# A batched matrix product on one core: what GpSimd's loads wait for, and who tells VectorE that a set of accumulators is done

## The chip, the cores and the metric

The kernel runs on one core of one Trainium2 chip. A core has several engines, each with its own program: TensorE (PE) multiplies, VectorE (DVE) and ScalarE (ACT) copy and convert here, GpSimd (POOL) and SyncE (SP) issue transfers. The engines meet only through semaphores: one engine counts a semaphore up, another waits until it has reached a value. Transfers between the chip's memory (DRAM) and the on-chip memory (SBUF) run on 16 DMA engines. Matrix products land in accumulators (PSUM banks). The metric is the time of one execution on the device in microseconds (us).

## What is computed

The reference multiplies 32 independent pairs of matrices:

```python
def setup_inputs():
    batch, m, k, n = 32, 512, 1024, 768
    return {
        "x": np.random.randn(batch, m, k).astype(np.float32),
        "weight": np.random.randn(batch, k, n).astype(np.float32),
    }

def reference(x, weight):
    return np.matmul(x, weight).astype(np.float32)
```

Per batch that is 2.10 MB of x, 3.15 MB of weights and 1.57 MB of output, all float32. The whole problem reads 167.77 MB and writes 50.33 MB. Every byte is moved once.

## The kernel before

The 32 batches go in 16 pairs. For each pair k the kernel loads x of both batches (one transfer, `load_x`, L108 to L112) and the weights of both (one transfer, `load_w`, L93 to L98; the first four and the last two batches one at a time, L102). These loads convert float32 to bfloat16 on the way into SBUF. There are two slots for x (`X_SLOTS`), four for weights (two pairs), and four for the output of a pair. Only x of pair 0 comes in float32, on SyncE's queue, and is converted by VectorE and ScalarE.

TensorE's loop (`on_pe`) does, for each pair: the transposes of x (`transposes`, eight groups `g` through two PSUM buffers `pt`), then for each of the two batches four row tiles `mt` of 128 rows (`multiply`). A row tile is 8 steps `ko`, and each step is two matmuls: one of 512 columns (L167) and one of 256 columns (L140). Two neighbouring row tiles, an even and an odd one, make a set: they share three PSUM banks, bank 0 (512 columns of the even tile), bank 2 (512 columns of the odd tile) and bank 1 (256 columns of each). There are two sets of banks, p = 0 and p = 1, so a batch is two sets and a pair is four. TensorE waits at L182 (`take`) for x (`s_xr`) and for weights (`s_wr`), and through `await_copies` for the copies that empty the banks (`s_a`, `s_d`).

ScalarE's program (`out_on_act`) copies, for each set: bank 0 in two pieces, after the even tile (L264 to L267), then half of bank 2, after the odd one (L268, L269). Between the two sets of an odd batch it waits until the next pair's x has landed and passes that on to TensorE (`landed`, L338). Before a pair it waits for its output slot (`slot_free`).

VectorE's program copies, for each set (`set_on_dve`, L271 to L276), bank 1 in two pieces, and then the other half of bank 2. It also spreads the transposed x from PSUM into SBUF (`spreads`, L224 or, for the last pair, L232). Its order is fixed in its loop: the eight spreads of pair k, then the second set of the last batch of pair k-1, then the other three sets of pair k. So the last copy of a pair stands behind the spreads of the next.

The semaphores that the change touches:

- `s_mm` counts finished tiles for ScalarE. Before, an even tile counts it at its last matmul (L171), and an odd tile at the last matmul of 512 columns (L170).
- `s_set` tells VectorE that a set is complete. Before, TensorE counts it at the last matmul of an odd tile (L171). VectorE waits for it at L272 and counts it down.
- `s_dp` counts VectorE's finished sets, two for each batch, and `s_ap` ScalarE's.

GpSimd's program (`on_pool`, L345 to L369) is one list in a fixed order: after the first loads, for k = 0 to 13: x of pair k+2, the store of pair k-2 (from k = 2 on), then the weights of pair k+2. All these transfers use one queue. Before, the load of x for pair k+2 waits (L111) until VectorE has finished the four sets of each pair before pair k (for k = 0: its first set), and the load of the weights (L96) until VectorE has finished pair k altogether. A wait on GpSimd holds all that stands behind it in the list. SyncE passes on the landed weights and does the last stores: pair 14 in one transfer, the last two batches in halves.

The functions that the change touches, with the line numbers of the profile:

Of the kernel before, what the change touches and what calls it, by code (L numbers as in the profile page):

```python
# [12 lines left out]
def kernel(  # L13
# [12 lines left out]
    KT = K // P  # L26
# [6 lines left out]
    W_SLOTS, X_SLOTS, OUT_SLOTS = 4, 2, 4  # L33

    pe, dve, act, pool, sp = nc.tensor, nc.vector, nc.scalar, nc.gpsimd, nc.sync
# [25 lines left out]
    def sem(name):  # L61
        sems.append(nc.alloc_semaphore(name))
        return sems[-1]
# [5 lines left out]
    s_pt, s_c, s_mm, s_set = sem("s_pt"), sem("s_c"), sem("s_mm"), sem("s_set")  # L69
    s_free = sem("s_free")  # L70
    s_a, s_ap, s_d, s_dp = sem("s_a"), sem("s_ap"), sem("s_d"), sem("s_dp")
    s_st = [sem(f"s_st{i}") for i in range(OUT_SLOTS)]
    s_fin = sem("s_fin")

    def out_done(b):
        return 2 * (b + 1)

    def out_before(k):  # L80
        return 4 * k

    def last_out(b):

# [5 lines left out]
    def together(b):  # L90
        return W_SLOTS <= b < B - 2

    def load_w(b):  # L93
        if together(b):
            if b % 2 == 0:
                pool.wait_ge(s_dp, out_done(b + 1 - W_SLOTS))  # L96
                slots = all_ws[:, b // 2 % 2].rearrange("p r ko n -> p r (ko n)")
                pool.dma_start(out=slots, in_=w_two_view[b // 2]).then_inc(s_w[b % W_SLOTS], 16)  # L98
            return
        if b >= W_SLOTS:  # L100
            pool.wait_ge(s_dp, out_done(b - W_SLOTS))
        pool.dma_start(out=ws[b % W_SLOTS], in_=w_view[b]).then_inc(s_w[b % W_SLOTS], 16)  # L102

    def loads_of_w(b):
# [2 lines left out]

    def load_x(k):  # L108
        if k >= X_SLOTS:

            pool.wait_ge(s_dp, max(out_before(k - X_SLOTS), 1))  # L111
        pool.dma_start(out=xs[k % X_SLOTS], in_=x_view[k]).then_inc(s_x[k % X_SLOTS], 16)  # L112

    def copied(eng, j):
# [14 lines left out]
    def stationary(b, mt):  # L129
        return both[mt][:, b % 2].rearrange("p j h i r -> p j (h i) r")  # L130
# [7 lines left out]
    def other(out, weights, moving, first, last):  # L138

        return pe.add_instruction(  # L140
            mybir.InstMatmult(
                name=nc.get_next_instruction_name(),
                engine=mybir.EngineType.PE,
                ins=[pe.lower_ap(moving), pe.lower_ap(weights)],
                outs=[pe.lower_ap(out)],
                start_tensor_calc=first,
                stop_tensor_calc=last,
                tile_size=(P, P),
                tile_position=(0, 0),
                ldweights=False,  # L150
            )
        )

    def multiply(b, mt, w):
        pm, half = pms[mt // 2], mt % 2
        xT = stationary(b, mt)
        for ko in range(KT):
            for i, (bank, at, off, size) in enumerate(SPLITS[half]):
                args = (
                    pm[bank][:, at:at + size],  # L160
                    xT[:, ko // 2, :, ko % 2],
                    w[:, ko, off:off + size],
                )
                if i:
                    last = other(*args, ko == 0, ko == KT - 1)
                else:
                    full = pe.matmul(*args, start=(ko == 0), stop=(ko == KT - 1))  # L167

        if half:
            full.then_inc(s_mm, 1)  # L170
        last.then_inc(s_set if half else s_mm, 1)  # L171

    def transpose(k, g):

# [21 lines left out]
    def on_pe():  # L196


        odd = pe.alloc_register("odd")
        pe.reg_mov(odd, 0)  # L200
        pe.wait_ge(s_ident, 1)
        with nc.Fori(0, PAIRS, engines=[mybir.EngineType.PE], hint_back_edge=True):
            take(s_xr)
            for k in range(X_SLOTS):
                with pe.If_eq(odd, k):
                    transposes(k)
            w_pair = all_ws[:, bass.ds(nc.snap(odd, min_val=0, max_val=1), 1)]
            for b in range(2):
                take(s_wr)
                for mt in range(MT):  # L210
                    if b == 0:
                        await_copies(s_c, 2 * mt + 2, GROUPS, GROUPS)
                    at = 2 * b + mt // 2 + 1 + mt % 2
                    await_copies(s_a, at, 5, 4)
                    await_copies(s_d, at, 5, 4)
                    multiply(b, mt, w_pair[:, 0, b])
            pe.reg_alu(odd, odd, 1, mybir.AluOpType.bitwise_xor)
# [17 lines left out]
    def slot_free(a):  # L235

        if a >= OUT_SLOTS:
            act.wait_ge(s_st[a % OUT_SLOTS], 16 * (a // OUT_SLOTS)).then_inc(s_free, 1)
# [8 lines left out]
    def pieces(b, p, i):  # L247

        pm = pms[p][i]
        if i == 1:  # L250
            pm = pm.rearrange("p (t n) -> p t n", t=2)
        rows = [slice(0, H), slice(H, P)]
        at = p * N2
        if b >= B - 2:
            return [(columns(last_out(b)[half, at:at + N2], i), pm[half]) for half in rows]
        mine = outs[(b // 2) % OUT_SLOTS][H * (b % 2):H * (b % 2 + 1)]
        starts = [at + h * ROW for h in range(2)]
        return [(columns(mine[:, at:at + N2], i), pm[half]) for at, half in zip(starts, rows)]

    def out_on_act(b, p):  # L260
        j = 2 * b + p
        if b % 2 == 0 and p == 0:
            slot_free(b // 2)
        act.wait_ge(s_mm, 2 * j + 1)  # L264
        for piece in pieces(b, p, 0):
            last = act.copy(*piece)  # L266
        last.then_inc(s_a, 1)  # L267
        act.wait_ge(s_mm, 2 * j + 2)  # L268
        act.copy(*pieces(b, p, 2)[0]).then_inc(s_ap, 1)  # L269

    def set_on_dve(b, p):  # L271
# [60 lines left out]
    def on_act():  # L332
        act.sem_inc(s_a, 2)
        cast_first(act, act.copy, range(MT, 2 * MT)).then_inc(s_xr, 1)
        for b in range(B):
            out_on_act(b, 0)
            if b % 2 and b < B - 1:
                landed(act, s_x[(b // 2 + 1) % X_SLOTS], (b // 2 + 2) // 2, s_xr)  # L338
            out_on_act(b, 1)
# [5 lines left out]
    def on_pool():  # L345
        load_w(0)
        pool.memset(ident, 0.0).then_inc(s_zero, 1)  # L347
        pool.wait_ge(s_zero, 1)
        pool.affine_select(  # L349
            out=ident,  # L350
            in_=ident,
            compare_op=mybir.AluOpType.not_equal,
            fill=1.0,
            base=0,
            pattern=[[-1, P]],
            channel_multiplier=1,
        ).then_inc(s_ident, 1)
        load_w(1)
        load_x(1)
        load_w(2)  # L360
        load_w(3)
        for k in range(PAIRS - 2):
            load_x(k + 2)
            if k >= 2:
                store(pool, k - 2, s_st[(k - 2) % OUT_SLOTS])
            load_w(2 * k + 4)
            load_w(2 * k + 5)
        for a in range(PAIRS - 2 - HELD, PAIRS - 2):
            store(pool, a, s_st[a % OUT_SLOTS])  # L369
# [59 lines left out]
```

## Time and profile before

| what | value |
|---|---|
| time, median of 3 runs | 517.16 us (516.54 to 518.05) |
| the profiled execution's own time | 517.05 us |
| its span (first to last instruction) | 515.3 us |
| mean granted clock of TensorE | 0.945 |
| TensorE busy with matmuls | 429.7 us (83%) |
| VectorE busy | 212.9 us (41%) |
| ScalarE busy | 116.4 us (23%) |
| GpSimd busy | 28.9 us (6%) |
| GpSimd's queue, share of the 16 DMA engines' time | 95.1% |
| weight loads of a pair, issue to landing (median) | 30.9 us |
| x loads, issue to landing (median) | 39.8 us |
| stores, issue to landing (median) | 47.0 us |

How to read the profile's lines. The page cuts the span into 40 slices; a digit is the busy share of a slice in tenths. A window's line gives the stretch in us, the sum of its length, the busy time of each engine (with the number of instructions), the clock granted to TensorE (1 is full speed), the share of time that the 16 DMA engines were busy, and the GB/s that they moved, counted as bytes written; a load that halves its data counts half of what it reads. The share can be a little over 1, as transfers overlap. A timeline's line gives the start and the length in us, the engine and the line of the kernel, the operation, what it writes and reads, how often, and in brackets how long the engine had been idle before it and what ended that. A line of waits names the waiting engine and line, what it waited for, the total in us, how many times, and the longest. PEq and DVEq are the instruction queues of TensorE and VectorE, and L182 and L272 the lines of the waits in them.

### The profile page before, as it was taken

To read this page: it belongs to the slowest core of one execution; us is meant where nothing else is said; L and a number is where in the kernel's file an instruction comes from. 1 tells how busy PE (TensorE), PEld (TensorE's weight loads), DVE (VectorE), ACT (ScalarE), POOL (GpSimd) and SP (SyncE) were. 2 spreads that over 40 slices of the span, in tenths; PEclk is the share of its full clock that TensorE was granted. 3 is DMA by queue.
4 is the path that set the end of the run, shared out by engine and by line. 5 is a ranking of instruction groups with operands and counts; after the bars stand their busy time and mean duration, and the time that the engine had idled before them with its cause. 6 is when DMAs were issued, how large, how long until landed. Compare 5 with 4: busy or idle time off the path is not lost. (4 is left out here: it accounts for less than half of the span.)

```text
span 515.3 us, 5719 instructions
## 1 busy us (share of the span) xinstructions
PE 429.7 (83%) x2512; PEld 174.5 (34%) x1536; DVE 212.9 (41%) x332; ACT 116.4 (23%) x197; POOL 28.9 (6%) x54
## 2 busy tenths in 40 slices
PE   0299999999896896979969699795997969879991
PEld 0143425352434233342433423333242343422420
DVE  0343736364545144362444514535244353533631
ACT  0313131313131230312303123130221303113130
POOL 2000001010100001001010000101001010010000
PEclk9999999999999897998989979998898989979996
DMA  8999998999999999999999999999999999999997
GB/s 297 258 215 224 191 220 175 219 243 292 219 336 223 270 276 225 331 222 298 250 221 336 214 322 232 230 324 217 337 217 257 298 221 335 222 264 283 344 433 293
DMA packets 9444, 136.36 MB, mean 265 GB/s; under 512 B 864, under 2 KB 864, under 8 KB 1376
## 3 DMA queue, kind: packets, MB, share of 16 engines
q0 software_dynamic: 8576, 125.83, 95.1%
q1 hardware_dynamic: 864, 10.49, 4.9%
q14 instruction: 3, 0.02, 0.0%
q8 instruction: 1, 0.02, 0.0%
HBM read 167.77 MB, written 50.33 MB: 423 GB/s over the span
## 5 line engine op out<-in xcount | busy, mean ns | idle before, releaser
L167 PE MATMUL pm<-w,xT 128*128 x976 | 335.6, 393 | 0.0
L140 PE MATMUL pm<-w,xT 128*128 x1024 | 287.4, 281 | 41.2 <-PEq L182 35.7
L167 PEld LDWEIGHTS pm<-w,xT 128*128 128x128 bf16 x1024 | 103.3, 101 | 280.5 <-issue 279.8
L274 DVE COPY outs<-pm 64x512 f32<-64x512 f32 x128 | 88.1, 689 | 206.1 <-DVEq L272 204.7
L266 ACT COPY outs<-pm 64x512 f32<-64x512 f32 x128 | 74.2, 580 | 285.4 <-PE pm L140 284.7
L178 PE MATMUL pt<-ident,x 128*128 128x128 f32 x512 | 84.9, 309 | 33.1 <-PEq L182 22.8
L224 DVE COPY xT<-pt 128x1024 bf16<-128x1024 bf16 x120 | 77.7, 687 | 64.4 <-PE pt L178 64.3
L178 PEld LDWEIGHTS pt<-ident,x 128*128 128x128 f32 x512 | 71.5, 210 | 48.4 <-issue 26.2
L269 ACT COPY outs<-pm 64x512 f32<-64x512 f32 x64 | 37.0, 578 | 85.3 <-PE pm L167 85.3
L276 DVE COPY outs<-pm 64x512 f32<-64x512 f32 x64 | 43.9, 687 | 0.0
L98 POOL DMA_DIRECT2D w<-in_weight_dram x13 | 9.2, 706 | 362.5 <-DVE outs L276 362.5
L284 DVE CAST x<-outs 128x1024 bf16<-128x1024 f32 x4 | 2.5, 686 | 18.6 <-DMA outs<-in_x_dram 18.6
L112 POOL DMA_DIRECT2D x<-in_x_dram x15 | 8.3, 556 | 32.8 <-DVE outs L276 32.8
L284 ACT CAST x<-outs 128x1024 bf16<-128x1024 f32 x4 | 3.9, 1040 | 16.3 <-DMA outs<-in_x_dram 16.3
L120 POOL DMA_DIRECT2D out_dram<-outs x14 | 7.5, 539 | 0.1
L232 DVE COPY xT<-pt 128x512 bf16<-128x512 bf16 x16 | 5.7, 417 | 4.1 <-PE pt L178 4.1
L102 POOL DMA_DIRECT2D w<-in_weight_dram x6 | 3.4, 566 | 29.9 <-DVE outs L276 28.7
L284 ACT ACT_TABLE_LOAD x1 | 1.3, 1283 | 1.0 <-ACTq L391 1.0
L349 POOL TENSOR_SCALAR_AFFINE_SELECT ident<-ident 128x128 f32<-128x128 f32 x1 | 0.3, 284 | 0.2 <-POOL ident L347 0.2
L347 POOL MEMSET ident<- 128x128 f32 x1 | 0.2, 224 | 0.0
L413 POOL MEMSET const-float32-0.0<- 128x1 f32 x1 | 0.1, 100 | 0.2 <-issue 0.2
L413 POOL MEMSET const-bfloat16-1.0<- 128x1 bf16 x1 | 0.1, 103 | 0.0
(2 smaller groups left out, 0.2 us busy)
## 6 DMA issues: line engine op xcount, KB each, us to landing
out_dram<-outs POOLq DMA_DIRECT2D x14, 3072.0 KB, 47.0
w<-in_weight_dram POOLq DMA_DIRECT2D x13, 3072.0 KB, 30.9
x<-in_x_dram POOLq DMA_DIRECT2D x15, 2048.0 KB, 39.8
w<-in_weight_dram POOLq DMA_DIRECT2D x6, 1536.0 KB, 36.3
outs<-in_x_dram SPq DMA_DIRECT2D x1, 4096.0 KB, 17.7
out_dram<-outs SPq DMA_DIRECT2D x1, 3072.0 KB, 18.6
out_dram<-outs SPq DMA_DIRECT2D x4, 768.0 KB, 12.3
```

The lines of the kernel that those rows point to most:

```text
L98: pool.dma_start(out=slots, in_=w_two_view[b // 2]).then_inc(s_w[b % W_SLOTS], 16)
L112: pool.dma_start(out=xs[k % X_SLOTS], in_=x_view[k]).then_inc(s_x[k % X_SLOTS], 16)
L120: eng.dma_start(out=two_view[a], in_=outs[a % OUT_SLOTS]).then_inc(sem, 16)
L140: return pe.add_instruction(mybir.InstMatmult(name=nc.get_next_instruction_name(), engine=mybir.EngineType.PE, ins=[pe.lower_ap(moving), p ...
L167: full = pe.matmul(*args, start=(ko == 0), stop=(ko == KT - 1))
L178: last = pe.transpose(pts[g % 2][:, j, :], words[:, mo, j::JT], ident)
L224: return dve.tensor_copy(both[g // 2][:, :, :, g % 2].rearrange("p b j i r -> p j b i r"), pt)
L266: last = act.copy(*piece)
L269: act.copy(*pieces(b, p, 2)[0]).then_inc(s_ap, 1)
L274: last = dve.tensor_copy(*piece)
L276: dve.tensor_copy(*pieces(b, p, 2)[1]).then_inc(s_dp, 1)
L284: last = copy(xs[0][:, mo], x_first[:, mo])
```

## The change

GpSimd's loads no longer wait for VectorE's count `s_dp` but for TensorE's count of row tiles, `s_mm`. The weights of a later batch wait until all four tiles of the batch that held the slot are multiplied (`mm_done`). The load of x for pair k+2 waits until the first tile of pair k is multiplied (`mm_begun`). The store's wait (`copied`) stays as it is.

For that, `s_mm` now counts each tile at its very last matmul, the odd ones too, and TensorE no longer counts `s_set`. ScalarE does so: its wait for the odd tile (the second wait in `out_on_act`) counts `s_set` up when it is met, ahead of its own copy. VectorE's wait for `s_set` is as before.

The order of the instructions on each engine stays the same, and so does the order of the transfers in each queue.

```diff
-    def out_done(b):
-        return 2 * (b + 1)
-
-    def out_before(k):
-        return 4 * k
+    def mm_done(b):
+        return 4 * (b + 1)
+
+    def mm_begun(k):
+
+        return 8 * k + 1
...
             if b % 2 == 0:
-                pool.wait_ge(s_dp, out_done(b + 1 - W_SLOTS))
+                pool.wait_ge(s_mm, mm_done(b + 1 - W_SLOTS))
...
         if b >= W_SLOTS:
-            pool.wait_ge(s_dp, out_done(b - W_SLOTS))
+            pool.wait_ge(s_mm, mm_done(b - W_SLOTS))
...
         if k >= X_SLOTS:
-
-            pool.wait_ge(s_dp, max(out_before(k - X_SLOTS), 1))
+            pool.wait_ge(s_mm, mm_begun(k - X_SLOTS))
...
                 else:
-                    full = pe.matmul(*args, start=(ko == 0), stop=(ko == KT - 1))
-
-        if half:
-            full.then_inc(s_mm, 1)
-        last.then_inc(s_set if half else s_mm, 1)
+                    last = pe.matmul(*args, start=(ko == 0), stop=(ko == KT - 1))
+        last.then_inc(s_mm, 1)
...
         last.then_inc(s_a, 1)
-        act.wait_ge(s_mm, 2 * j + 2)
+
+        act.wait_ge(s_mm, 2 * j + 2).then_inc(s_set, 1)
         act.copy(*pieces(b, p, 2)[0]).then_inc(s_ap, 1)
```

## The prediction

> **What bounds the kernel now.** I read the page's slices and queue table first, to see which resource is always busy, then the waits, to see who lacks data, then the windows, to see whether the transfers ever stop, and last GpSimd's timeline, to see why. The slices and the queue of GpSimd's transfers:
>
> ```profile
> PE   0299999999896896979969699795997969879991
> ...
> DMA  8999998999999999999999999999999999999997
> ...
> q0 software_dynamic: 8576, 125.83, 95.1%
> ...
> HBM read 167.77 MB, written 50.33 MB: 423 GB/s over the span
> ```
>
> DMA is full in 37 of 40 slices and TensorE isn't. The waits agree:
>
> ```profile
> POOL w L98 <- DVE outs L276: 362.5, 13, 31.7
> ...
> PE pm L140 <- PEq L182: 35.7, 9, 5.5
> ...
> PE pm L140 <- DVE outs L274: 2.4, 1, 2.4
> ```
>
> TensorE stops nine times at L182 for weights (35.7 us); for VectorE's copies it stops once. GpSimd's long wait is only the time until a slot comes free. It costs something only if the queue runs empty meanwhile, so the windows decide:
>
> ```profile
> 56.00:60.00 4.00, 3.95 (x26) 1.58 (x16) 3.29 (x6) 0.55 (x1) 0.12 (x1) 1.00 1.15 246
> 60.00:64.00 4.00, 4.00 (x26) 1.18 (x12) 1.82 (x3) 1.20 (x3) 1.13 (x2) 1.00 0.83 140
> 64.00:68.00 4.00, 3.95 (x25) 1.25 (x13) 0.80 (x2) 1.74 (x3) 0.00 (x0) 1.00 0.98 209
> ...
> 80.00:84.00 4.00, 3.42 (x22) 2.57 (x20) 3.51 (x6) 0.00 (x0) 0.00 (x0) 1.00 1.09 233
> 84.00:88.00 4.00, 4.00 (x26) 1.18 (x12) 2.01 (x4) 1.16 (x2) 1.64 (x3) 1.00 0.74 130
> 88.00:92.00 4.00, 3.95 (x25) 1.22 (x13) 1.98 (x3) 1.28 (x3) 0.15 (x1) 1.00 0.82 169
> ...
> 164.00:456.00 292.00, 247.25 (x1419) 99.06 (x868) 120.25 (x184) 62.58 (x108) 18.25 (x31) 0.92 1.02 265
> ...
> 508.00:510.00 2.00, 0.00 (x0) 0.00 (x0) 0.00 (x0) 0.00 (x0) 0.00 (x0) 0.50 0.98 406
> ```
>
> The last two columns are the DMA share and GB/s. Loads run at about 213 GB/s (they count what they write, half of what they read). From 164 us on the share is 1.02: no gap. But at 60-64 and 84-92 the rate drops while TensorE is fully busy. GpSimd's timeline shows why:
>
> ```profile
> 59.88 0.71 POOL L98 DMA_DIRECT2D w<-in_weight_dram  x1 [21.35 <-DVE outs L276]
> 60.57 0.56 POOL L112 DMA_DIRECT2D x<-in_x_dram  x1
> ...
> 86.36 0.71 POOL L98 DMA_DIRECT2D w<-in_weight_dram  x1 [25.23 <-DVE outs L276]
> 87.06 0.56 POOL L112 DMA_DIRECT2D x<-in_x_dram  x1
> ```
>
> The weight load and the next x load go out together, just as the queue has emptied. So the kernel is DMA-bound with two holes, both early.
>
> **Size of the holes.** By bytes against 213 GB/s: 60-64 lacks (213-140)/213 x 4 = 1.4 us; 84-92 lacks (426-299)/213 x 4 = 2.4 us; together 3.8. Taking in the fast rows beside them (56-68: 595 of 639, 0.8 us; 80-96 with 230 in its last row: 762 of 852, 1.7 us) gives 2.5. A third way: in the steady part GpSimd's weight issues go from 166.74 to 422.02 in eight pairs, 31.9 us for 13.63 MB (6.29 of weights, 4.19 of x, 3.15 of output), or 427 GB/s. Between 59.88 and 86.36 only weights and x flow (no store yet): 10.49 MB, 24.6 us of 26.5, so 1.9 us are empty; with 1.1 to 1.4 us at 60 this gives 3.0 to 3.3. I take 3.3, inside 2.5 to 3.8.
>
> **Part 1: the weight loads wait for TensorE.** Before, the load for pair k+2 needs VectorE's count of pair k, whose last copy stands in VectorE's program behind the eight spreads of pair k+1:
>
> ```profile
> 50.98 1.12 PE L178 MATMUL pt<-ident,x 128*128 128x128 f32 x8
> ...
> 56.26 1.29 DVE L224 COPY xT<-pt 128x1024 bf16<-128x1024 bf16 x2 [0.24 <-PE pt L178]
> ...
> 58.89 0.69 DVE L276 COPY outs<-pm 64x512 f32<-64x512 f32 x1
> ...
> 454.10 0.42 PE L140 MATMUL pm<-w,xT 128*128 x1 [4.05 <-PEq L182]
> ...
> 504.10 1.39 DVE L274 COPY outs<-pm 64x512 f32<-64x512 f32 x2 [3.20 <-DVEq L272]
> ```
>
> After, it needs the last multiplication of pair k, which ends where the transposes begin: 51.0 instead of 59.88, 8.9 us sooner (and 77.5 instead of 86.36). The order of transfers in the queue stays the same. At 51.0 the four first weight loads and x(1) (20.97 MB with x(0), 49 us at 427 from 2 us on) are about done and x(2), 9.8 us, is left, so the weights follow it at about 60.5 without a hole. They take 14.7 us, to 75. At 77.5 x(3) is running (to 85) and the next weights stand behind it: the second hole goes too. Later there is no hole to fill and the sooner issue is worth 0. Gain: 3.3 us. The two single loads at the end, now issued 2.1 us (two of VectorE's piece copies) and some 9 us sooner, have the same queue ahead of them: 0.
>
> **Part 2: the x loads wait for the pair's first tile.** A tile is 8 pairs of matmuls 0.33 us apart, 2.6 us; pair 1's first ends at 56.87 + 2.6 = 59.5 against the issue at 60.57, so a microsecond sooner; x(2) goes from 37.99 to 30.4 + 2.6 = 33. Where TensorE has waited for weights it is later: at 454.10 its matmuls are 0.64 us apart (clock 0.5), so a first tile there ends at 459.2, against VectorE's count at 453.1: 6 us later, and the store behind it on GpSimd too. When the weights of a pair land, the queue still holds x (9.8), a store (7.4) and, by part 1, the next weights (14.7): 31.9 us. 6 us late costs 0; without that cover it would cost up to 6 us in each of the 9 waits.
>
> **Part 3: ScalarE passes the set on.** One increment per set moves from TensorE to ScalarE, 64 of them; no instruction is added to an engine's compute. VectorE starts later by one more semaphore step. Such steps show as 0.15 us (last matmul ends 503.95, VectorE starts 504.10) to 0.30 us (transposes after a spread); I take 0.2, as 0.19 is the common one. ScalarE could also be late, but its two copies (2 x 0.58) are done 1.3 us before the tile ends. What waits for VectorE's set is TensorE, a tile later: 2.6 - 0.15 - 1.39 = 1.06 us of room, which covers 0.2. After the spreads the set's flag is long up. At the end 0.2 us lies on the last copies, but the stores behind them still drain at full rate (406 GB/s at 508-510), so 0 to 0.3; I take 0. ScalarE's second copy now waits for the smaller matmul as well, 0.1 us, covered in the same way. No gain is in it, since VectorE waited for the same two matmuls before.
>
> **Part 4: GpSimd issues beside VectorE's spreads.** Before, each waiting issue comes right after the copy that released it; none lies inside a run of spreads. Bounds: 0, or a hold until the run and the set behind it are over, 8.6 us (51.0 to 59.6). I take 0: a held issue needs only to go out within the 9 us that x(2) still takes, and VectorE leaves gaps of 0.24 us.
>
> **Sum.** The profiled execution took 517.05 us, 0.11 below the median of 517.16, with a span of 515.3. TensorE's last two pairs start from weights that land 3.3 us sooner, and the last stores have 3.3 us less ahead of them, so the end moves with the queue: 517.05 - 3.3 + 0 = 513.75, say 513.8.
>
> **The rivals.** (a) No change, about 517. GpSimd's issue is held while VectorE spreads, until about 59.6: both holes stay. Against it: the gaps between the spreads, and that these copies read PSUM. For it: no row shows an issue there.
> The Trainium skill, SBUF — State Buffer, section Who interferes with whom, says that VectorE in a two-port mode shuts GpSimd out while it writes a transfer's descriptors; by that alone the gain would be 0 and the time 517. Its VectorE: DVE Perf Modes, section Why PSUM operands drop a tier, says that a copy out of PSUM never uses that mode, which would leave the gain; no row of this trace tests either.
> (b) Slower. TensorE begins to wait for VectorE. Its room is 1.06 us; if the relay through ScalarE took 1.5 us instead of 0.2, it would lose 0.44 us at two tiles of each batch. Earlier pairs have weight waits of up to 5.5 us that swallow this, but the last two pairs (8 such tiles, nearly no spare TensorE time from 454 to 504) would end 3.5 us later, which eats the 3.3 us. So a relay of 1.5 us decides; at 2.2 us the loss is 8 x 1.14 = 9.1 and the time 513.8 + 9.1 = 522.9. Against it: no semaphore step in the trace exceeds 0.30.
> (c) Much faster: TensorE's 35.7 us of waiting go, 517.05 - 35.7 = 481. That would take 218.1 MB in under 480 us, 455 GB/s, where the steady part gives 427.
>
> **How the numbers follow.** Forecast 0.80, rival (a) 0.12, (b) 0.06, (c) 0.02. About 0.3%, 1.6 us, is what a measurement of this kernel can tell from no change; the forecast's own range is 512.4 (3.8 us of holes and the runs' spread of some 0.8 us) to 515.4 (2.5 us, and the same spread). All of it counts as faster: 0.82 with (c); same 0.12; slower 0.06. To hold 8 in 10 the range reaches into (a): 512.2 to 516.8.
>
> **What would show it.** In the windows, 60-64 and 84-92 should read over 200 GB/s; the weight issues should stand at about 51 and 77 us, released by TensorE's L140; the first wait of TensorE at L182 (169.2 now) should end near 166; VectorE's sets should start 0.1 to 0.3 us after ScalarE's wait; the share should stay near 1.0 from then on. The prediction is wrong if the holes close and the end doesn't move (then the stores or TensorE's last pairs set it), if issues inside the spreads take longer than 0.71 us, or if TensorE's waits for VectorE grow beyond 2.4 us.

## The result and the profile after

The changed kernel takes 513.54 us (median of 6 runs, 512.87 to 514.15). The kernel before, run beside it, takes 517.20 us. The ratio is 0.9927 with a 95% interval of 0.9913 to 0.9942, so the change saves 3.8 us (3.0 to 4.5). The forecast was 513.8. The profiled execution took 513.18 us with a span of 511.1.

The page of the changed kernel, its slices, GpSimd's queue and the rate over the span:

```profile
PE   0299999999998986969989599896998969889990
...
DMA  8999999999999999999999999999999999999997
...
q0 software_dynamic: 8576, 125.83, 95.5%
...
HBM read 167.77 MB, written 50.33 MB: 427 GB/s over the span
```

The same bytes and packets move; they only move in a shorter span, 427 GB/s against 423. The seventh slice of the DMA row, at 77 to 90 us, read 8 before and reads 9 now.

The windows of the changed kernel at the two holes and at the end (the last two columns are the DMA share and GB/s):

```profile
60.00:64.00 4.00, 4.00 (x26) 1.25 (x13) 1.87 (x3) 1.11 (x2) 0.18 (x1) 1.00 0.95 201
...
84.00:88.00 4.00, 4.00 (x27) 1.21 (x13) 1.95 (x3) 1.16 (x2) 1.10 (x2) 1.00 1.03 217
88.00:92.00 4.00, 4.00 (x27) 1.24 (x13) 1.98 (x3) 1.37 (x3) 0.00 (x0) 1.00 1.04 221
...
504.00:508.00 4.00, 0.00 (x0) 0.00 (x0) 0.00 (x0) 0.00 (x0) 0.00 (x0) 0.50 0.88 367
508.00:512.00 4.00, 0.00 (x0) 0.00 (x0) 0.00 (x0) 0.00 (x0) 0.00 (x0) 0.50 0.06 25
```

Where 140, 130 and 169 GB/s stood, there are now 201, 217 and 221. A third stretch changes too, which lies between the windows that the prediction shows. The first line is of the kernel before, the second of the changed kernel:

```profile
112.00:116.00 4.00, 4.00 (x27) 1.20 (x13) 1.40 (x4) 1.74 (x3) 1.80 (x3) 1.00 0.77 295
...
112.00:116.00 4.00, 4.00 (x27) 1.18 (x12) 1.35 (x3) 1.74 (x3) 1.09 (x2) 1.00 0.96 412
```

GpSimd's timeline shows why the first two holes close. The weight loads go out 8.5 us sooner, released by TensorE, while earlier loads still move data (213, 197 and 258 GB/s in the three windows from 48 to 60 us):

```profile
51.35 0.71 POOL L98 DMA_DIRECT2D w<-in_weight_dram  x1 [17.66 <-PE pm L139]
59.62 0.56 POOL L111 DMA_DIRECT2D x<-in_x_dram  x1 [7.57 <-PE pm L139]
77.83 0.70 POOL L98 DMA_DIRECT2D w<-in_weight_dram  x1 [17.65 <-PE pm L139]
```

The waits of the changed kernel:

```profile
POOL w L98 <- PE pm L139: 224.6, 13, 17.7
...
PE pm L166 <- PEq L178: 29.5, 9, 4.9
...
PE pm L166 <- DVE outs L271: 2.3, 1, 2.3
```

TensorE still stops nine times for weights by the profile (L178 is the line that was L182), 29.5 us instead of 35.7, and once for VectorE. That last one is a wait for weights too, before and after the change. It ends at 327.87 in the kernel before and at 385.42 in the changed one, and these times fill the one gap in a row of weight waits that end 31 to 32 us apart (296.27 and 359.53 before, 353.61 and 417.41 after). It stands at the first tile of a pair, which by the program needs no copy later than VectorE's third set of the pair before. In the changed kernel the bank 1 copies of that set ended at 373.8, long before. So TensorE waits ten times for weights, 38.1 us before and 31.8 after, and no new wait took the old one's place. Its timeline gives the first and last of these waits, the one at 385.42, and the last copies of VectorE:

```profile
164.31 0.39 PE L166 MATMUL pm<-w,xT 128*128 x1 [1.37 <-PEq L178]
...
385.42 0.39 PE L166 MATMUL pm<-w,xT 128*128 x1 [2.29 <-DVE outs L271]
...
448.90 0.60 PE L166 MATMUL pm<-w,xT 128*128 x1 [3.15 <-PEq L178]
...
498.12 1.39 DVE L271 COPY outs<-pm 64x512 f32<-64x512 f32 x2 [3.20 <-DVEq L269]
499.43 0.69 DVE L273 COPY outs<-pm 64x512 f32<-64x512 f32 x1
```

The first wait now ends at 164.31 instead of 169.20. The last ends at 448.90 instead of 454.10, and the last copy ends at 500.1 instead of 506.1. The span shrank by only 4.2, which the experiments take up.

### The profile page after: what moved, and what is told of

Its sections match the earlier page's. It is cut to its first block, busy times and chain, and to the rows that moved or that the text cites. A ratio compares the mean times of both kernels' runs of the same rounds, so it can differ in the third digit from the quotient of the medians.

```text
span 511.1 us, 5831 instructions
## 1 busy us (share of the span) xinstructions
PE 433.1 (85%) x2560; PEld 174.0 (34%) x1536; DVE 212.9 (42%) x332; ACT 116.4 (23%) x197; POOL 29.1 (6%) x54
## 5 line engine op out<-in xcount | busy, mean ns | idle before, releaser
L166 PE MATMUL pm<-w,xT 128*128 x1024 | 349.1, 392 | 31.8 <-PEq L178 29.5
L139 PE MATMUL pm<-w,xT 128*128 x1024 | 286.2, 279 | 0.0
```

The costliest lines, as they stand in the source:

```text
L139: return pe.add_instruction(mybir.InstMatmult(name=nc.get_next_instruction_name(), engine=mybir.EngineType.PE, ins=[pe.lower_ap(moving), p ...
L166: last = pe.matmul(*args, start=(ko == 0), stop=(ko == KT - 1))
```

## The experiments

The working theory is that the gain comes from the two weight loads at 60 and 86 us, which close the holes there, and from nothing else. The rivals are that it came from the sooner x loads, from ScalarE's relay, or from sooner loads later in the run or at its end, since VectorE's last copies moved by 6 us. In the diffs a line with minus is that of the changed kernel, dots stand for lines left out, and the lines that bring back `out_done` and `out_before` are left out. The ratios are to the kernel before, run beside each (medians 517.1 to 517.4 us).

### One part at a time

The weight loads alone on TensorE's count:

```diff
 def load_x(k):
-    pool.wait_ge(s_mm, mm_begun(k - X_SLOTS))
+    pool.wait_ge(s_dp, max(out_before(k - X_SLOTS), 1))
```

> The change with the x loads put back on VectorE's count; the weight loads stay on TensorE's. Holes theory (the gain is the two stretches at 60 and 86 us in which the queue was empty): both stay closed, 513.5 us (513.0 to 514.2). If the sooner x loads made the gain: 517.

Measured: 513.48 us, ratio 0.9921 (0.9905 to 0.9936). All of the gain is there without the x loads.

The x loads alone:

```diff
 def load_w(b):
-    pool.wait_ge(s_mm, mm_done(b + 1 - W_SLOTS))
+    pool.wait_ge(s_dp, out_done(b + 1 - W_SLOTS))
...
-    pool.wait_ge(s_mm, mm_done(b - W_SLOTS))
+    pool.wait_ge(s_dp, out_done(b - W_SLOTS))
```

> The change with the weight loads put back on VectorE's count; the x loads stay on TensorE's. Holes theory: GpSimd's list holds x(3) behind the weights of pair 2 at 59.9 us, so both holes stay: 517 us (516.5 to 517.8). If the x loads made the gain: 513.5.

Measured: 517.74 us, ratio 1.0003 (0.9993 to 1.0013). GpSimd's timeline of this run:

```profile
32.64 0.53 POOL L117 DMA_DIRECT2D x<-in_x_dram  x1 [27.42 <-PE pm L145]
59.27 0.70 POOL L104 DMA_DIRECT2D w<-in_weight_dram  x1 [26.10 <-DVE outs L279]
59.97 0.56 POOL L117 DMA_DIRECT2D x<-in_x_dram  x1
```

The first x load goes out some 5 us sooner and gains nothing: in the kernel before, the transfers already ran at 197 and 203 GB/s in the windows from 36 to 44 us. The next stands in GpSimd's list behind the weights and goes when they go, and both holes stay (146 GB/s at 60-64, 128 at 84-88).

ScalarE's relay alone, with both edits above:

> All loads put back on VectorE's count; only ScalarE's passing on of the set is left of the change. Holes theory: 517.2 us, no difference from the kernel before (within 0.2%). If TensorE's saved count or ScalarE's relay made part of the gain: below 516.

Measured: 517.20 us, ratio 0.9996 (0.9984 to 1.0008). The relay neither gains nor costs anything that can be measured.

### Which of the weight loads

Only the loads at 60 and 86 us (batches 4 and 6) keep TensorE's count:

```diff
 def load_w(b):
-    pool.wait_ge(s_mm, mm_done(b + 1 - W_SLOTS))
+    if b in (4, 6):
+        pool.wait_ge(s_mm, mm_done(b + 1 - W_SLOTS))
+    else:
+        pool.wait_ge(s_dp, out_done(b + 1 - W_SLOTS))
...
```

The x loads and the last two weight loads go back to `s_dp`, as above.

> Only the weight loads of pairs 2 and 3 (the ones at 60 and 86 us) wait for TensorE's count; all later weight loads, the last two single ones and all x loads wait for VectorE's. Holes theory: the whole gain, 513.5 us (513.0 to 514.2). If the gain comes from sooner loads later in the run or at its end (the rival: the last copies of VectorE begin 6 us sooner, the span only shrinks by 4.2): 516 to 517.

Measured: 513.31 us, ratio 0.9924 (0.9906 to 0.9942). Two of the 15 changed weight loads make the whole gain. The other 13, the last two among them, add nothing that can be measured. The third stretch closes with them: 112-116 reads 406 GB/s here, although the weight load there goes out as late as before (113.11 us).

With `(4,)` in that list, and then with `(6,)`:

> Only the weight load of pair 2 (at 60 us) waits for TensorE's count, all others as before the change. Holes theory: hole one closes, but the queue then empties that much sooner before the load at 86 us, so hole two grows by as much: 517 us, no gain. If each hole has its own price: 515.5.

Measured: 517.03 us, ratio 1.0000 (0.9989 to 1.0012).

> Only the weight load of pair 3 (at 86 us) waits for TensorE's count, all others as before the change. Holes theory: hole one stays, hole two closes: a gain of 2 to 3 us, 514.3 to 515.3 us. If the two loads count alike (each its own price): the same time as with the first one alone.

Measured: 515.25 us, ratio 0.9959 (0.9944 to 0.9975). The windows, of the run with the first load alone:

```profile
60.00:64.00 4.00, 4.00 (x27) 1.20 (x13) 1.97 (x3) 1.01 (x2) 0.23 (x1) 1.00 0.94 199
84.00:88.00 4.00, 4.00 (x27) 1.23 (x13) 1.85 (x3) 1.16 (x2) 1.79 (x3) 1.00 0.51 75
```

and of the run with the second load alone:

```profile
60.00:64.00 4.00, 4.00 (x27) 1.23 (x13) 1.94 (x3) 1.04 (x2) 0.96 (x2) 1.00 0.88 153
84.00:88.00 4.00, 4.00 (x27) 1.25 (x13) 1.87 (x3) 1.16 (x2) 1.09 (x2) 1.00 0.93 197
```

Closing the first hole alone moves it: 84-88 falls from 130 to 75 GB/s, because the queue empties sooner while the load that refills it comes at the same time (86.16 us there). Closing the second alone removes it and leaves the first. The two loads are worth 0, 2.1 and 3.9 us (ratios 1.0000, 0.9959 and 0.9924 of 517) as the first, the second and both. They don't add up, which a queue that must not run empty explains and a price per load does not.

### A hole made on purpose

The x loads wait until the whole pair is multiplied, so that x and weights come at once:

```diff
 def load_x(k):
-    pool.wait_ge(s_mm, mm_begun(k - X_SLOTS))
+    pool.wait_ge(s_mm, mm_done(2 * (k - X_SLOTS) + 1))
```

> The change, but the x load of pair k+2 waits until all of pair k is multiplied, so x and weights go out together at the end of a pair. Holes theory: the queue is empty when they go out at about 51, 78 and 104 us; each hole is about 0.8 us of emptiness and 1.5 us to start again, so three holes add 7 us: 520.5 us (517.5 to 523), with TensorE busy in all of them. If empty stretches this early don't set the end: 513.5.

Measured: 520.07 us, ratio 1.0051 (1.0033 to 1.0069), 6.5 us above the changed kernel. The windows show the three holes, with TensorE at work in each (the first lies across two windows):

```profile
48.00:52.00 4.00, 4.00 (x28) 1.91 (x17) 0.47 (x2) 1.74 (x3) 0.51 (x1) 1.00 0.71 151
52.00:56.00 4.00, 3.33 (x22) 2.72 (x20) 3.51 (x6) 0.00 (x0) 0.73 (x2) 1.00 0.97 172
76.00:80.00 4.00, 3.70 (x27) 2.47 (x20) 1.57 (x3) 0.85 (x2) 1.28 (x2) 1.00 0.75 129
104.00:108.00 4.00, 3.51 (x24) 3.02 (x23) 2.69 (x5) 0.58 (x1) 1.80 (x3) 1.00 0.68 113
```

So a hole of about 2 us early in the run is about 2 us at its end. The sum is rough, as a fourth thin stretch follows at 116-120 (a DMA share of 0.71). This run also answers rival (a). Its second pair of loads goes out at 77.96 and 78.52 into an empty queue, just as VectorE begins a run of spreads (78.19 to about 84). The windows of that stretch, 1 us each:

```profile
77.00:78.00 1.00, 1.00 (x10) 0.70 (x7) 0.00 (x0) 0.21 (x1) 0.04 (x1) 1.00 0.25 49
78.00:79.00 1.00, 0.70 (x7) 0.51 (x5) 0.81 (x2) 0.37 (x1) 1.00 (x2) 1.00 0.00 0
79.00:80.00 1.00, 1.00 (x8) 0.96 (x8) 0.76 (x2) 0.00 (x0) 0.24 (x1) 1.00 1.71 246
80.00:81.00 1.00, 0.82 (x7) 0.63 (x5) 1.00 (x2) 0.00 (x0) 0.00 (x0) 1.00 0.19 33
81.00:82.00 1.00, 0.82 (x6) 0.58 (x6) 0.76 (x3) 0.00 (x0) 0.00 (x0) 1.00 1.15 246
```

Data flows again from 79 on, a microsecond after the issue and 5 us before VectorE is through. The dip at 80-81 needs no VectorE either: in the kernel before, the rate after the second hole falls in the same way, to 49 and 25 GB/s from 88 to 89 us, and there VectorE is idle until 88.8. So the spreads did not hold the loads.

### Is it the queue alone?

Half of the matmuls are left out, and all transfers stay:

```diff
 def multiply(b, mt, w):
-    for ko in range(KT):
+    for ko in range(0, KT, 2):
...
```

The dots stand for the flag that ends the sum, which moves to the last step that is left.

> The change with every second step of the sum left out of the multiplication (4 of 8, so half of TensorE's matmuls); all transfers, transposes and copies stay. Queue theory: 218.1 MB at the 432 GB/s of the steady part is 505 us, with start and end about 510 us (507 to 513). If TensorE's work set the time: some 150 us less.

Measured: 513.38 us, ratio 0.9923 (0.9905 to 0.9940): the time of the changed kernel, with half the multiplication. TensorE's waits for weights grow to fill the space, and VectorE's last copy ends at 490.5, 20 us before the end of the span (510.8):

```profile
PE pm L139 <- PEq L178: 150.9, 14, 12.7
...
489.83 0.69 DVE L273 COPY outs<-pm 64x512 f32<-64x512 f32 x1
```

So the multiplications don't set the time, not even those of the last two pairs. What does is the queue of transfers, from about 2 us to the last store.

### The relay made longer

ScalarE raises the flag only after its own copy of bank 2:

```diff
-        act.wait_ge(s_mm, 2 * j + 2).then_inc(s_set, 1)
+        act.wait_ge(s_mm, 2 * j + 2)
         act.copy(*pieces(b, p, 2)[0]).then_inc(s_ap, 1)
+        act.wait_ge(s_ap, j + 1).then_inc(s_set, 1)
```

> The change, but ScalarE tells VectorE's loop only after its own copy of bank 2: the relay grows from 0.1 to about 0.75 us. The prediction's room of 1.06 us covers it: no new waits of TensorE for VectorE's L271, 513.5 us (513.0 to 514.2). If there is no such room: 8 tiles of the last two pairs lose 0.6 us each, 517.

Measured: 514.26 us, ratio 0.9939 (0.9916 to 0.9962). The median is a little above the expected range, but its interval takes in the changed kernel's 0.9927, so a cost of a few tenths can be neither shown nor excluded. VectorE starts 0.77 us after ScalarE's copy begins. The profile puts three waits of TensorE down to VectorE, 6.8 us in all, but they end at 228.67, 324.15 and 420.06, again in gaps of the row of weight waits. The short waits inside a pair that the next run shows are missing here, which agrees with a room of more than 0.77 us.

With the same copy done three times, one after the other, before the flag:

> The change, but ScalarE tells VectorE's loop only after three copies of bank 2, one after the other (two of them repeat work): a relay of about 2.2 us, rival (b)'s figure. By the room of 1.06 us TensorE waits about 1.1 us at some four tiles of each pair; up to pair 13 this comes out of its waits for weights, in the last two pairs it adds 9 us to the multiplication and the relay 2 us behind it, of which the stores still draining hide about 4: 520.5 us (518 to 523). If the relay never matters: 513.5.

Measured: 517.46 us, ratio 1.0002 (0.9993 to 1.0012), below the expected range. The waits, the end of TensorE's and VectorE's timelines, and the last windows:

```profile
PE pm L167 <- DVE outs L276: 30.7, 32, 1.0
...
PE pm L167 <- PEq L183: 15.4, 16, 1.0
...
498.62 0.38 PE L167 MATMUL pm<-w,xT 128*128 x1 [0.96 <-DVE outs L276]
...
509.73 1.39 DVE L276 COPY outs<-pm 64x512 f32<-64x512 f32 x2 [4.33 <-DVEq L274]
511.04 0.69 DVE L278 COPY outs<-pm 64x512 f32<-64x512 f32 x1
...
504.00:508.00 4.00, 2.76 (x16) 0.78 (x8) 1.39 (x3) 1.41 (x3) 0.00 (x0) 1.00 0.83 343
508.00:512.00 4.00, 0.00 (x0) 0.00 (x0) 1.98 (x3) 1.48 (x3) 0.00 (x0) 0.88 0.20 80
512.00:516.00 4.00, 0.00 (x0) 0.00 (x0) 0.00 (x0) 0.00 (x0) 0.00 (x0) 0.50 0.48 197
```

The room is what the prediction said. The relay here is 1.98 us (ScalarE's last such copies begin at 507.75, VectorE at 509.73), 1.06 less is 0.92, and TensorE waits 0.96 us at the tile. Both lines of waits are of this kind (L183 is the wait for copies in `await_copies`): three tiles of each pair, 48 in all and 46.1 us, where the expectation had four tiles. The 40 us of them before pair 14 are more than the waits for weights that they replace, so pair 14 begins to multiply at 453.49 instead of 448.90. Six waits in the last two pairs and the longer relay at the end follow. But of the 11.6 us by which the last copy is late (511.7 against 500.1) only 4.9 show in the span (516.0 against 511.1). The stores all but ran empty at 508-512 and the span ended 4.3 us after the last copy. In the changed kernel it ends 11.0 us after. So 6.7 us of room lay between the last copy and the end there, where 4 were expected.

## Why the prediction was right

**The bound** was read rightly: the queue, with holes early in the run. With half the matmuls left out the time is the same, and the two loads at the holes make all of the gain. The waits were misread in one point: the stop "for VectorE's copies" is a tenth wait for weights. The forecast does not rest on it, but the sign of being wrong that names 2.4 us of waits for VectorE does: that figure was no wait for VectorE at all.

The prediction's windows also leave out the time from 96 to 164 us. In the kernel before, no data moves from 112.5 to 113.5, although a store had been issued at 87.61. So this stretch is not a late issue like the other two, and why it is there stays open. It goes when the two early holes go.

**The size of the holes** was low by some tenths. The sum took 3.3 us, and both loads together gave 3.9 us (3.0 to 4.9), so the miss is within the noise. The second hole was put at 1.9 by the issue times and measured 2.1 (1.3 to 2.9); the first was put at 1.1 to 1.4, and 3.9 - 2.1 leaves 1.8. The first was given no row for its 1.1. The byte count without the neighbouring rows, 3.8, was nearest, but nothing in the prediction singled it out. No term stood for the stretch at 112-116; how much of the difference it makes up is not shown.

**Part 1** held in its mechanism: weights at 51.35 and 77.83 (51.0 and 77.5 forecast), no hole, and the later loads and the last two worth 0.

**Part 2** held: the x loads alone gave 1.0003. Its example at 454.10 stands behind the last x load (422.71) and so concerns none, but the delay it describes is there: in the steady part of the run with the x loads alone they go out up to 6.6 us behind the weights, where before they followed at once, and it cost nothing.

**Part 3** held. The relay adds less than the 0.2 us taken: before, VectorE's last set began 0.15 us after the last matmul ended; now it begins 0.20 us after (matmul to 497.92, VectorE at 498.12), 0.08 after ScalarE's copy starts. The room of 1.06 us was confirmed by the threefold copy.

**Part 4** held. An issue in a run of spreads moves data after about a microsecond. The Trainium skill, SBUF — State Buffer, section Who interferes with whom, lets an instruction of VectorE in a two-port mode shut GpSimd out as long as that instruction lasts, not for a whole run of them, as the prediction's bound has it. The Trainium skill, VectorE: DVE Perf Modes, section Why PSUM operands drop a tier, exempts copies out of PSUM. The run with the x loads at the pair's end agrees with the exemption: 246 GB/s at 79-80 beside copies that read PSUM.

**The sum's last sentence** was half right. It let the end move because TensorE's last two pairs start sooner and because the stores have less ahead of them. Only the second counts: with VectorE's last copies 20 us ahead of the end the time was the same. VectorE's 6 us are therefore not a gain that was lost. That TensorE's first wait ends 4.9 us sooner while the span shrinks by 4.2 is chance for the most part. In the four traces at the time before (before, x loads alone, relay alone, first load alone) it ends at 169.20, 168.22, 168.58 and 168.48; in four at the changed kernel's time (after, weight loads alone, two loads, half the products) at 164.31, 164.56, 165.05 and 164.59. The means are 4.0 us apart, and those of the spans 3.9.

**Rival (b)'s price** was too high. The step "at 2.2 us the loss is 8 x 1.14 = 9.1 and the time 513.8 + 9.1 = 522.9" let every microsecond of the multiplication through to the end. The run gave 517.46: the relay was 1.98 us, not 2.2, the loss fell on six tiles of 0.96 us in the last two pairs, not on eight of 1.14, the waits for weights of the earlier pairs did not swallow all of theirs (pair 14 began 4.6 us later), and the stores still to be drained hid 6.7 us. Its turning point moves accordingly: a relay of 1.98 us brings the kernel only back to the time before, where 1.5 was to do that.

## What to carry to other kernels

In a kernel that is bound by one queue of transfers, an earlier issue is worth about the time for which the queue would have run short, and nothing where a backlog stands; look for windows where the rate falls while the compute engines are busy, and for late issues in them. Such a hole is not tied to a load: closing the first alone pushed it to the next late issue here, so all have to be closed up to the point where the backlog lasts. A wait that the profile puts down to one engine is worth holding against the program and against the times of its neighbours. Before pricing a delay of the last computation, look at how long the stores still run after it.

## What the runs showed that was not expected

With the threefold copy TensorE's mean granted clock rose to 0.992, from 0.955 in the changed kernel: its short waits of 0.96 us, spread over the run, left hardly a wait for weights. After the one that is left, of 2.0 us, the windows read 0.79 and 0.78; before the change, after one of 5.5 us, the window at 168-172 reads 0.50. With half the products it fell to 0.825 and the time didn't change. In a run bound by its transfers the clock says how the idle time is spread, not how fast the kernel is.
